# A transformer block on one core: w_up's activations scaled on VectorE, halves evacuated one by one, and new waiting counts

## The chip, the core and the metric

The kernel runs on one core of a Trainium2 chip. A core has a matrix engine (TensorE, PE in the profile, with its weight loads as PEld), VectorE (DVE), ScalarE (ACT), GpSimd (POOL) and SyncE (SP), which issues most of the DMAs. Each engine works through its own list of instructions in order and waits for others by semaphores. The metric is device time in microseconds for one execution; less is better.

## The reference

One block at batch 1, 256 rows, width 1024, all in float32:

```python
h = rms_norm(x, norm_mix_g);  proj = h @ w_in          # pool part u, and q, k, v of 8 heads
x = x + concat([pool_mixer(u), attention(rope(norm(q)), rope(norm(k)), v)]) @ w_out
h = rms_norm(x, norm_xattn_g);  m = rms_norm(mem, norm_mem_g)
x = x + cross_attention(h, m)                          # 4 heads of 256, w_xq, w_xkv, w_xo
h = rms_norm(x, norm_ffn_g)                            # x * rsqrt(mean(x*x) + eps) * g
up = causal_conv3(h @ w_up, conv_w) + conv_b           # w_up: 1024 x 5632, 3 taps along the rows
gate, val = split(up);  x = x + (silu(gate) * val) @ w_down      # 2816 -> 1024
```

## The kernel before

**Precision and tiles.** Every matrix product is done on pairs: a float32 operand is split into a high part, rounded by a copy on ScalarE (`split_h` for weights, `part_h` for activations), and the rest, which VectorE gets by a subtraction (`split_l`, `part_l`). Weights come in units of 128 x 1024; one unit is one output tile of 128 columns over 8 blocks of 128 inputs. `need(u)` is called in front of a unit's matmuls: it emits ScalarE's cast of unit u + look + 1 and VectorE's split of unit u + look; look is 4 while w_up is worked on and 1 in w_down's stage. `b_tile` makes one output tile transposed (128 features x 256 rows): `both` multiplies each block's high weights with both halves of the activation (512 columns) and its low weights with the high half (256 columns), so that a PSUM bank holds two halves that still have to be added. `three` does the same as three matmuls of 256 columns into one half. There are 8 banks.

**The order of work.** Nothing is scheduled by a machine: engines get instructions in the order in which Python emits them. The matmuls are emitted in a straight line, and everything else is in generators (`go` starts one). `tick()` advances every running generator by one `yield`; `b_tile` ticks three times in a tile of 8 blocks, the loops once more after it. The tables WAIT_... at the head of the file say how many ticks a job lets pass between its stages, and so where its instructions stand among the others. `finish(job)` ticks until a job is done.

**w_up and w_down.** 22 pairs (gate tile g = 0, value tile g = 1) make 44 tiles, each 8 blocks. The first 3 pairs use the activations without the row scale 1/rms (`h2`) and are multiplied by it later (`r2b`, a 128 x 256 tile with the scale of each row); from pair SCALED = 3 on the tiles use `hs2`, which `r2_job` makes while the first pairs run: GpSimd multiplies a block of the residual by `r2b`, ScalarE makes the high part and VectorE the low part with the gain g, 8 times. After a pair's two tiles `up_job` copies the second half of each bank on ScalarE (L928) and adds the first half on VectorE (L929), which gives `up`. ScalarE then starts the convolution (`y`, two instructions, L938), VectorE adds the other two taps (four instructions, L945; they are called the taps below), ScalarE takes silu, VectorE multiplies gate and value (L951), and the product is split into `act` (L253 on ScalarE, L259 on VectorE). w_down's tile f then runs over 22 blocks, one for each pair, and waits for that pair's `act`. Its two halves are added to the residual on VectorE (L989) and stored.

**Keys.** `qk_job` turns the projected keys by rope, computes a scale per head (`rsqrt`, a chain on GpSimd), scales the keys on VectorE (L453) and transposes them on TensorE (L460).

Of the kernel before, what the change touches and what calls it, by code (L numbers as in the profile page):

```python
# [13 lines left out]
ALU = mybir.AluOpType  # L14
# [4 lines left out]
S = 256  # L19
# [20 lines left out]
WAIT_MEAN = [0]  # L40
WAIT_STAT = [2, 14, 8, 0, 0, 30]
WAIT_ROPE = [6, 6, 0]
WAIT_QK = [12, 12, 8, 25, 0, 2]
WAIT_V = [2, 10]
WAIT_MEM = [2, 2]
WAIT_SCORE = [5, 4, 0, 9, 1, 6]
# [3 lines left out]
WAIT_R1 = [6]  # L50
WAIT_X = [3, 0, 0, 0, 10, 0, 6, 13, 8]
WAIT_VALUE = [32]
WAIT_R2 = [6, 6, 1, 1, 0]
WAIT_LOW = [2]
WAIT_UP = [6, 2, 5, 7, 9, 8]
SCALED = 3
WARM = 10


C_GMIX, C_X = 0, KT  # L60
# [17 lines left out]
def block_kernel(ctx: ExitStack, tc: tile.TileContext, wpack: bass.AP, xpack: bass.AP, scal: bass.AP,  # L78
# [189 lines left out]
    def three(o, stat, mov, start, stop):  # L268
# [2 lines left out]
        pe.matmul(o, stat[0], mov[1], start=False, stop=False)  # L271
        pe.matmul(o, stat[1], mov[0], start=False, stop=stop)  # L272

    def both(b, stat, mov, start, stop):

        n = mov.shape[1] // 2
        if start:
            pe.matmul(b, stat[0], mov, start=True, stop=False)  # L278
            pe.matmul(b[:, 0:n], stat[1], mov[:, 0:n], start=False, stop=False)  # L279
        else:  # L280
            pe.matmul(b[:, 0:n], stat[1], mov[:, 0:n], start=False, stop=False)  # L281
            pe.matmul(b, stat[0], mov, start=False, stop=stop)  # L282

    def col(t, c):
        return t[:, c:c + 1]
# [80 lines left out]

    def first_splits():
        for k in range(KT):
            part_h(xgv[0][:, k], resid[:, k], col(sc, C_GMIX + k))
            part_l(xgv[1][:, k], resid[:, k], xgv[0][:, k], col(sc, C_GMIX + k))  # L370
            r = slice(k % 2 * 512, k % 2 * 512 + 512)
            split_h(k // 2, r, dve.tensor_copy if k == 0 else act.copy)
            split_l(k // 2, r)
        next_split[0] = FIRST

# [2 lines left out]
    def a_chunk(u0, actv, bk):  # L378

        for k in range(KT):  # L380
            w = need(u0 + k // 2)
            wv = [t[:, (k % 2) * 512:(k % 2) * 512 + 512] for t in w]
            a = [[t[:, k, tt * P:(tt + 1) * P] for t in actv[:2]] for tt in range(TT)]
            for tt in range(TT):
                pe.matmul(bk[tt], a[tt][0], wv[0], start=k == 0, stop=False)  # L385
                pe.matmul(bk[tt], a[tt][1], wv[0], start=False, stop=False)  # L386
            tick()
            for tt in range(TT):
                pe.matmul(bk[tt], a[tt][0], wv[1], start=False, stop=k == KT - 1)  # L389
            tick()  # L390
# [330 lines left out]

    def b_tile(u0, f, blocks, b, mov):

        for k in range(blocks):
            i = f * blocks + k
            w = need(u0 + i // 8)
            wv = [t[:, (i % 8) * P:(i % 8 + 1) * P] for t in w]
            both(b, wv, mov(k), k == 0, k == blocks - 1)
            halves[0] += 1
            if halves[0] % 2 == 0 and k < blocks - 1:  # L730
                tick()
# [168 lines left out]
    def r2_job():  # L900

        yield from wait(WAIT_R2[0])
        v2 = yield from row_mean(acc2, "2")
        r2 = rsqrt(v2, TT, True)
        yield from wait(WAIT_R2[1])
        b = bank()
        for tt in range(TT):
            pe.matmul(b[:, tt * P:(tt + 1) * P], col(r2, tt).to_broadcast([P, P]), ident, start=True, stop=True)
        yield from wait(WAIT_R2[2])
        dve.tensor_copy(r2b, b[:, 0:S])  # L910
        r2_ready.append(True)
        yield from wait(WAIT_R2[3])
        prev = None
        for k in range(KT + 1):
            if prev is not None:
                part_h(hs2[0][:, k - 1], prev, col(sc, C_GFFN + k - 1))
                part_l(hs2[1][:, k - 1], prev, hs2[0][:, k - 1], col(sc, C_GFFN + k - 1))
            if k < KT:
                t = t1(f"hs{k}")
                pool.tensor_tensor(t, resid[:, k], r2b, op=ALU.mult)  # L920
                prev = t
            yield from wait(WAIT_R2[4])

    def up_job(i, bs, scaled):
        src = t2(f"up{i}")
        for g in range(2):
            half = src[:, g * S:(g + 1) * S]
            act.copy(half, bs[g][:, S:])  # L928
            dve.tensor_tensor(half, bs[g][:, 0:S], half, op=ALU.add)  # L929
        if not scaled:  # L930
            while not r2_ready:
                yield
            src2 = src.rearrange("p (g s) -> p g s", g=2)
            dve.tensor_tensor(src2, src2, r2b[:, None, :].to_broadcast([P, 2, S]), op=ALU.mult)
        y = t2(f"y{i}")
        for g in range(2):
            f = i + g * NFF
            act.activation(y[:, g * S:(g + 1) * S], src[:, g * S:(g + 1) * S], AF.Identity, bias=col(sc, C_CB + f),  # L938
                           scale=col(sc, C_CW + 2 * 2 * NFF + f))
        yield from wait(WAIT_UP[1])  # L940
        for j in (1, 2):
            for g in range(2):
                f = i + g * NFF
                uu, yy = src[:, g * S:(g + 1) * S], y[:, g * S:(g + 1) * S]
                dve.scalar_tensor_tensor(yy[:, j:], uu[:, :S - j], col(sc, C_CW + (2 - j) * 2 * NFF + f), yy[:, j:],  # L945
                                         op0=ALU.mult, op1=ALU.add)
        yield from wait(WAIT_UP[2])
        sg = t2(f"sg{i}")
        act.activation(sg[:, 0:S], y[:, 0:S], AF.Silu)
        yield from wait(WAIT_UP[3])  # L950
        dve.tensor_tensor(sg[:, S:], sg[:, 0:S], y[:, S:], op=ALU.mult)  # L951
        yield from wait(WAIT_UP[4])
        h, l = (t[:, i % 8] for t in acts[i // 8][:2])
        part_h(h, sg[:, S:])
        yield from wait(WAIT_UP[5])
        part_l(l, sg[:, S:], h)

    job_r2 = []
    jobs_up = []
    look[0] = LOOKS[10]  # L960
    for i in range(NFF):
        bs = [bank(), bank()]
        if i == 0:
            hs2 = tiles(pair("hs2"), KT, S)
            job_r2.append(go(r2_job()))
        scaled = i >= SCALED
        hv = hs2 if scaled else h2
        if i == SCALED:
            finish(job_r2[0])
        for g in range(2):  # L970
            b_tile(58, 2 * i + g, KT, bs[g], lambda k: hv[2][:, k])
# [10 lines left out]

    look[0] = LOOKS[11]
    for f in range(KT):
        b = bank()
        b_tile(102, f, NFF, b, act_tile)
        o = t2(f"o{f}")[:, 0:S]
        for z, add in enumerate((resid[:, f], o)):
            dve.tensor_tensor(o, b[:, z * S:(z + 1) * S], add, op=ALU.add)  # L989
        nc.sync.dma_start(out[:, f], o)  # L990

# [98 lines left out]
```

## Time and profile before

| | |
|---|---|
| time, median of 3 runs | 390.47 us (390.45 to 392.52) |
| the profiled execution: its time, and the span of its instructions | 390.8 us, 389.0 us |
| TensorE busy | 381.3 us, 98% of the span |
| VectorE busy | 313.3 us, 81% |
| ScalarE busy | 248.2 us, 64% |
| GpSimd busy | 77.1 us, 20% |
| DMA | 69.14 MB, mean 178 GB/s |

The span runs from the first to the last instruction of the profile. Busy time is the union of an engine's instruction times. Instructions of one engine overlap a little, so that two in a row take less than the sum of their durations; the start of one to the start of the next is what the engine can keep up.

### The profile page before, as it was taken

The page shows a single profiled execution, that of the slowest core. Times are in us where ns is not written, and L with a number is a line of the kernel's source. Part 1 is how long each engine was busy: PE and PEld are TensorE (multiplying, and loading weights), DVE is VectorE, ACT ScalarE, POOL GpSimd, SP SyncE. Part 2 cuts the span into 40 slices and gives each one's busy share as a digit, 9 for nine tenths or more (in the row PEclk, how much of TensorE's full clock was granted, in tenths as well). Part 3 has the DMA queues.
Part 4 walks back from the last instruction along what each step waited for, and adds up shares of the span by engine and source line. Part 5 has one row for each costly group of instructions (what it writes and reads, how often), then busy time and mean ns, then how long its engine had stood idle before and what let it go on. Part 6 is the DMA issues. An engine that isn't in the chain of part 4 may idle for free.

```text
span 389.0 us, 5984 instructions
## 1 busy us (share of the span) xinstructions
PE 381.3 (98%) x2178; PEld 328.7 (84%) x2178; DVE 313.3 (81%) x562; ACT 248.2 (64%) x475; POOL 77.1 (20%) x160
## 2 busy tenths in 40 slices
PE   8999899999999999999999999999999999999995
PEld 8888688888888988898888878888888888888884
DVE  4769899978879859678978989999999998654460
ACT  5775797977557747745655678778877777442210
POOL 0272786142832122100325100000000000000000
PEclk9999999999999999999999999999999999999999
DMA  8985381453505624363535055555655554364400
GB/s 281 423 329 192 134 305 67 176 211 110 199 19 216 217 108 190 135 217 109 189 125 231 1 155 204 196 211 209 218 216 202 184 191 181 124 241 166 186 19 21
DMA packets 12269, 69.14 MB, mean 178 GB/s; under 512 B 1360, under 2 KB 2768, under 8 KB 4688
## 3 DMA queue, kind: packets, MB, share of 16 engines
q1 hardware_dynamic: 11952, 68.24, 47.5%
q10 hardware_dynamic: 288, 0.52, 0.4%
q8 instruction: 17, 0.28, 0.3%
q14 instruction: 12, 0.10, 0.1%
HBM read 67.71 MB, written 1.05 MB: 177 GB/s over the span
## 4 chain that ended last, share of the span: by engine, by line
PE 79%; DVE 9%; DMA 3%; ACT 3%; issue 2%; POOL 2%; SPq 0%; DVEq 0%
PE bank L282 34%; PE bank L281 17%; PE bank L385 5%; PE bank L386 5%; PE bank L389 5%; PE bank L278 4%; DVE wl L205 3%; PE bank L279 2%; DMA raw<-wpack 2%; DVE hs L261 2%; DMA sc<-xpack 1%; PE bank L272 1%; PE bank L271 1%; PE bank L270 1%; ACT wh L194 1%
## 5 line engine op out<-in xcount | busy, mean ns | idle before, releaser
L205 DVE TENSOR_TENSOR wl<-raw,wh 128x1024 fp32r<-128x1024 f32 (+1 forms) x126 | 149.3, 1202 | 3.1 <-ACT wh L194 3.1
L194 ACT CAST wh<-raw 128x1024 fp32r<-128x1024 f32 (+1 forms) x125 | 123.6, 1022 | 36.0 <-DMA raw<-wpack 35.0
L282 PE MATMUL bank<-hs,wh 128*128 128x512 f32 x266 | 94.8, 396 | 0.0
L281 PE MATMUL bank<-hs,wl 128*128 128x256 f32 x266 | 74.2, 279 | 0.0
L282 PE MATMUL bank<-act,wh 128*128 128x512 f32 x168 | 59.6, 398 | 0.0
L282 PEld LDWEIGHTS bank<-hs,wh 128*128 128x128 f32 x266 | 49.9, 188 | 10.3
L281 PEld LDWEIGHTS bank<-hs,wl 128*128 128x128 f32 x266 | 50.1, 189 | 1.6
L281 PE MATMUL bank<-act,wl 128*128 128x256 f32 x168 | 47.1, 281 | 0.0
L938 ACT ACTIVATE y<-up,sc 128x256 f32<-128x256 f32 x44 | 24.1, 595 | 27.0 <-DVE up L929 19.7
L282 PEld LDWEIGHTS bank<-act,wh 128*128 128x128 f32 x168 | 31.6, 188 | 7.4
L945 DVE SCALAR_TENSOR_TENSOR y<-up,sc,y 128x255 f32<-128x255 f32 (+1 forms) x88 | 36.6, 477 | 0.3 <-ACT y L938 0.3
L282 PE MATMUL bank<-h,wh 128*128 128x512 f32 x98 | 35.1, 396 | 0.0
L281 PEld LDWEIGHTS bank<-act,wl 128*128 128x128 f32 x168 | 31.7, 189 | 0.3
L281 PE MATMUL bank<-h,wl 128*128 128x256 f32 x98 | 27.6, 281 | 0.0
L989 DVE TENSOR_TENSOR o<-bank,sc 128x256 f32<-128x256 f32 x8 | 3.4, 425 | 29.4 <-PE bank L282 29.4
L385 PE MATMUL bank<-wh,mg 128*128 128x512 f32 x64 | 26.1, 408 | 0.0
L385 PE MATMUL bank<-wh,xg 128*128 128x512 f32 x64 | 26.0, 406 | 0.0
L386 PE MATMUL bank<-wh,xg 128*128 128x512 f32 x64 | 25.4, 397 | 0.0
L386 PE MATMUL bank<-wh,mg 128*128 128x512 f32 x64 | 25.1, 392 | 0.0
L747 POOL TENSOR_TENSOR h_acc<-h_sq,h_acc 128x256 f32<-128x256 f32 x14 | 13.4, 956 | 43.3 <-ACT h_sq L746 43.1
L282 PEld LDWEIGHTS bank<-h,wh 128*128 128x128 f32 x98 | 18.4, 188 | 3.6
L255 ACT ACTIVATE h<-sc 128x256 fp32r<-128x256 f32 x16 | 8.2, 511 | 20.5 <-DVE sc L739 20.4
(256 smaller groups left out, 770.1 us busy)
## 6 DMA issues: line engine op xcount, KB each, us to landing
raw<-wpack SPq DMA_DIRECT2D x59, 1024.0 KB, 4.8
raw<-wpack SPq DMA_DIRECT2D x4, 512.0 KB, 7.8
mraw<-memT SPq DMA_DIRECT2D x4, 256.0 KB, 6.8
out<-o SPq DMA_DIRECT2D x8, 128.0 KB, 1.9
raw<-wpack ACTq DMA_DIRECT2D x2, 256.0 KB, 3.5
raw<-wpack SPq DMA_DIRECT2D x2, 256.0 KB, 4.8
sc<-xpack SPq DMA_DIRECT2D x1, 512.0 KB, 6.4
tab<-table SPq DMA_DIRECT2D x1, 480.0 KB, 9.1
```

The costliest lines, as they stand in the source:

```text
L194: copy(split[u][0][:, r], unit(u)[:, r])
L205: dve.tensor_tensor(l[:, r], unit(u)[:, r], h[:, r].bitcast(F32), op=ALU.subtract)
L255: act.activation(h, src, AF.Copy, scale=scale)
L278: pe.matmul(b, stat[0], mov, start=True, stop=False)
L281: pe.matmul(b[:, 0:n], stat[1], mov[:, 0:n], start=False, stop=False)
L282: pe.matmul(b, stat[0], mov, start=False, stop=stop)
L385: pe.matmul(bk[tt], a[tt][0], wv[0], start=k == 0, stop=False)
L386: pe.matmul(bk[tt], a[tt][1], wv[0], start=False, stop=False)
L389: pe.matmul(bk[tt], a[tt][0], wv[1], start=False, stop=k == KT - 1)
L747: pool.tensor_tensor(acc, sq, acc, op=ALU.add)
L938: act.activation(y[:, g * S:(g + 1) * S], src[:, g * S:(g + 1) * S], AF.Identity, bias=col(sc, C_CB + f), scale=col(sc, C_CW + 2 * 2 * NFF ...
L945: dve.scalar_tensor_tensor(yy[:, j:], uu[:, :S - j], col(sc, C_CW + (2 - j) * 2 * NFF + f), yy[:, j:], op0=ALU.mult, op1=ALU.add)
```

## The change

It has six parts. (1) In the first splits the cast of a weight part stands ahead of the activation's low part, the first projection's matmuls alternate between the two banks, and 8 instead of 10 idle matmuls warm TensorE. (2) The keys are scaled 3 ticks later and transposed 5 ticks later. (3) `r2_job` makes hs2's products on VectorE, with scale and gain in one instruction, in pairs of blocks; ScalarE and VectorE then split 512 columns at once. (4) Each half of a pair is evacuated by a generator of its own, `up_half`, as soon as its tile is done, and VectorE's addition stands two ticks behind ScalarE's copy. (5) `up_job` starts 2 ticks later and its taps come 3 ticks after `y` instead of 2; the last three pairs have short pauses. (6) w_down's last tile uses `three`, so that one addition is left at the end.

```diff
-WAIT_QK = [12, 12, 8, 25, 0, 2]
+WAIT_QK = [12, 14, 11, 25, 0, 2]
-WAIT_R2 = [6, 6, 1, 1, 0]
+WAIT_R2 = [6, 6, 1, 0, 1]
-WAIT_UP = [6, 2, 5, 7, 9, 8]
+WAIT_UP = [6, 3, 5, 7, 9, 8]
+WAIT_LAST = [0, 1, 2, 1, 2, 1]
+N_LAST = 3
-WARM = 10
+WARM = 8
...
+            split_h(k // 2, r, dve.tensor_copy if k == 0 else act.copy)
             part_l(xgv[1][:, k], resid[:, k], xgv[0][:, k], col(sc, C_GMIX + k))
-            split_h(k // 2, r, dve.tensor_copy if k == 0 else act.copy)
             split_l(k // 2, r)
...
             for tt in range(TT):
                 pe.matmul(bk[tt], a[tt][0], wv[0], start=k == 0, stop=False)
+            for tt in range(TT):
                 pe.matmul(bk[tt], a[tt][1], wv[0], start=False, stop=False)
...
-        prev = None
-        for k in range(KT + 1):
-            if prev is not None:
-                part_h(hs2[0][:, k - 1], prev, col(sc, C_GFFN + k - 1))
-                part_l(hs2[1][:, k - 1], prev, hs2[0][:, k - 1], col(sc, C_GFFN + k - 1))
-            if k < KT:
-                t = t1(f"hs{k}")
-                pool.tensor_tensor(t, resid[:, k], r2b, op=ALU.mult)
-                prev = t
-            yield from wait(WAIT_R2[4])
+        for j in range(KT // 2):
+            ts.append(t2(f"hs{j}").rearrange("p (k s) -> p k s", k=2))
+            for k in range(2):
+                dve.scalar_tensor_tensor(ts[j][:, k], resid[:, 2 * j + k], col(sc, C_GFFN + 2 * j + k), r2b,
+                                         op0=ALU.mult, op1=ALU.mult)
+            part_h(hs2[0][:, 2 * j:2 * j + 2], ts[j])
+        yield from wait(WAIT_R2[4])
+        for j in range(KT // 2):
+            part_l(hs2[1][:, 2 * j:2 * j + 2], ts[j], hs2[0][:, 2 * j:2 * j + 2])
...
+    def up_half(o, b):
+        act.copy(o, b[:, S:])
+        yield from wait(WAIT_LOW[0])
+        dve.tensor_tensor(o, b[:, 0:S], o, op=ALU.add)
+
+    def up_job(i, src, scaled):
+        pause = WAIT_LAST if i >= NFF - N_LAST else WAIT_UP
+        yield from wait(WAIT_LOW[0])
-        src = t2(f"up{i}")
-        for g in range(2):
-            half = src[:, g * S:(g + 1) * S]
-            act.copy(half, bs[g][:, S:])
-            dve.tensor_tensor(half, bs[g][:, 0:S], half, op=ALU.add)
...
         for g in range(2):
-            b_tile(58, 2 * i + g, KT, bs[g], lambda k: hv[2][:, k])
+            b = bank()
+            b_tile(58, 2 * i + g, KT, b, lambda k: hv[2][:, k])
+            go(up_half(up[:, g * S:(g + 1) * S], b))
             if g == 0:
                 tick()
-        jobs_up.append(go(up_job(i, bs, scaled)))
+        jobs_up.append(go(up_job(i, up, scaled)))
         tick()
...
-        b = bank()
-        b_tile(102, f, NFF, b, act_tile)
+        last = f == KT - 1
+        b = bank()[:, 0:S] if last else bank()
+        b_tile(102, f, NFF, b, (lambda k: halves_of(act_tile(k))) if last else act_tile)
```

**VectorE in w_up's stage.** One pair's worth of VectorE's list in the middle of the stage, before (`up` is the pair's sum of halves, `wl` a split of weights, `y` the taps, `sg` the gated product, `act` its low part; the numbers tell buffers apart):

```order
L929 TENSOR_TENSOR up_2650<-bank_2596,up_2650 128x256
L929 TENSOR_TENSOR up_2650<-bank_2597,up_2650 128x256
L205 TENSOR_TENSOR wl_2662<-raw_2502,wh_2625 128x1024
L945 SCALAR_TENSOR_TENSOR y_2655<-up_2650,sc,y_2655 128x255 x2
L945 SCALAR_TENSOR_TENSOR y_2655<-up_2650,sc,y_2655 128x254 x2
L205 TENSOR_TENSOR wl_2688<-raw_2502,wh_2660 128x1024
L951 TENSOR_TENSOR sg_2640<-sg_2640,y_2593 128x256
L259 TENSOR_TENSOR act_2311<-sg_2517,act_2311 128x256
```

The same stretch in the changed kernel:

```order
L935 TENSOR_TENSOR up_2575<-bank_2576,up_2575 128x256
L961 TENSOR_TENSOR sg_2586<-sg_2586,y_2528 128x256
L208 TENSOR_TENSOR wl_2640<-raw_2490,wh_2612 128x1024
L262 TENSOR_TENSOR act_2313<-sg_2464,act_2313 128x256
L935 TENSOR_TENSOR up_2575<-bank_2609,up_2575 128x256
L955 SCALAR_TENSOR_TENSOR y_2651<-up_2575,sc,y_2651 128x255 x2
L955 SCALAR_TENSOR_TENSOR y_2651<-up_2575,sc,y_2651 128x254 x2
L208 TENSOR_TENSOR wl_2676<-raw_2490,wh_2638 128x1024
```

The instructions are the same ten. Before, a weight split stood between the second addition and the taps; now the taps stand directly behind the second addition, and both splits lie elsewhere. ScalarE's `y` stands between addition and taps in the dependencies, in both kernels.

**VectorE where hs2 is made.** Before, from the copy of `r2b` on (six more hs rows follow, then the taps of pair 0):

```order
L205 TENSOR_TENSOR wl_2346<-raw_2160,wh_2319 128x1024
L910 COPY r2b<-bank_2339 128x256
L934 TENSOR_TENSOR up_2312<-up_2312,r2b 128x512
L261 SCALAR_TENSOR_TENSOR hs_2245<-hs_2361,sc,hs_2245 128x256
L261 SCALAR_TENSOR_TENSOR hs_2245<-hs_2365,sc,hs_2245 128x256
```

And in the changed kernel:

```order
L918 COPY r2b<-bank_2338 128x256
L925 SCALAR_TENSOR_TENSOR hs_2353<-sc,r2b 128x256 x2
L925 SCALAR_TENSOR_TENSOR hs_2357<-sc,r2b 128x256 x2
L925 SCALAR_TENSOR_TENSOR hs_2361<-sc,r2b 128x256 x2
L925 SCALAR_TENSOR_TENSOR hs_2365<-sc,r2b 128x256 x2
L944 TENSOR_TENSOR up_2241<-up_2241,r2b 128x512
L935 TENSOR_TENSOR up_2314<-bank_2315,up_2314 128x256
L262 TENSOR_TENSOR hs_2242<-hs_2353,hs_2242 128x2x256
L262 TENSOR_TENSOR hs_2242<-hs_2357,hs_2242 128x2x256
```

The eight products now stand on VectorE itself, and the low parts are four instructions of 512 columns (two more follow) instead of eight of 256.

**VectorE at the keys.** Before (`m1k` are the keys, `rs1y` their scale, `m2q` a product of the queries' rope):

```order
L205 TENSOR_TENSOR wl_416<-raw_244,wh_396 128x1024
L226 TENSOR_SCALAR rs2y<-vx 128x2
L453 TENSOR_TENSOR m1k_271<-m1k_271,rs1y 128x512
L453 TENSOR_TENSOR m1k_276<-m1k_276,rs1y 128x512
L427 TENSOR_TENSOR m2q_385<-bank_281,ropeq 128x8x32 x2
L427 TENSOR_TENSOR m2q_390<-bank_282,ropeq 128x8x32 x2
L205 TENSOR_TENSOR wl_456<-raw_299,wh_414 128x1024
```

And now:

```order
L208 TENSOR_TENSOR wl_414<-raw_242,wh_394 128x1024
L229 TENSOR_SCALAR rs2y<-vx 128x2
L434 TENSOR_TENSOR m2q_383<-bank_279,ropeq 128x8x32 x2
L434 TENSOR_TENSOR m2q_388<-bank_280,ropeq 128x8x32 x2
L208 TENSOR_TENSOR wl_452<-raw_297,wh_412 128x1024
L460 TENSOR_TENSOR m1k_269<-m1k_269,rs1y 128x512
L460 TENSOR_TENSOR m1k_274<-m1k_274,rs1y 128x512
```

The keys' scaling has moved behind the queries' four products and a weight split. On TensorE the keys' transposes stand 16 matmuls of 512 columns later than before, two matmuls ahead of the queries'.

## Rows read from the trace of the kernel before

**Rows 1.** Waits of TensorE: engine line, waited for: total us, times, longest.

```profile
PE bank L460 <- DVE m1k L453: 1.4, 1, 1.4
PE bank L279 <- DVE wl L205: 1.0, 1, 1.0
```

**Rows 2.** Windows: stretch, length, busy us (PE, PEld, DVE, ACT, POOL), PEclk, DMA share, GB/s.

```profile
240.00:324.00 84.00, 84.00 (x482) 73.16 (x482) 84.00 (x163) 66.48 (x130) 0.00 (x0) 1.00 0.55 201
```

**Rows 3.** Timeline, VectorE and ScalarE, one pair: start us, us, what, [idle <-releaser].

```profile
313.88 0.75 DVE L929 TENSOR_TENSOR up<-bank,up 128x256 f32<-128x256 f32 x2
314.33 1.10 ACT L938 ACTIVATE y<-up,sc 128x256 f32<-128x256 f32 x2 [1.05 <-DVE up L929]
315.68 1.66 DVE L945 SCALAR_TENSOR_TENSOR y<-up,sc,y 128x255 f32<-128x255 f32 x4
319.06 0.75 DVE L929 TENSOR_TENSOR up<-bank,up 128x256 f32<-128x256 f32 x2
```

**Rows 4.** Timeline of several engines, from hs2's making to pair 3's taps.

```profile
208.58 7.06 POOL L920 TENSOR_TENSOR hs<-sc,r2b 128x256 f32<-128x256 f32 x8 [7.60 <-DVE r2b L910]
210.79 5.92 DVE L261 SCALAR_TENSOR_TENSOR hs<-hs,sc,hs 128x256 fp32r<-128x256 f32 x8 [1.56 <-ACT hs L255]
220.35 0.40 PE L278 MATMUL bank<-hs,wh 128*128 128x512 f32 x1
225.03 0.76 DVE L929 TENSOR_TENSOR up<-bank,up 128x256 f32<-128x256 f32 x2 [1.50 <-ACT up L928]
227.70 0.38 PE L279 MATMUL bank<-hs,wl 128*128 128x256 f32 x1 [0.96 <-DVE wl L205]
232.74 1.67 DVE L945 SCALAR_TENSOR_TENSOR y<-up,sc,y 128x255 f32<-128x255 f32 x4
```

**Rows 5.** Timeline where w_up ends: last pair, and w_down's first tile.

```profile
322.92 0.40 PE L278 MATMUL bank<-act,wh 128*128 128x512 f32 x1
324.70 1.09 ACT L938 ACTIVATE y<-up,sc 128x256 f32<-128x256 f32 x2 [1.05 <-DVE up L929]
325.33 1.77 DVE L945 SCALAR_TENSOR_TENSOR y<-up,sc,y 128x255 f32<-128x255 f32 x4 [0.34 <-ACT y L938]
328.02 1.09 DVE L259 TENSOR_TENSOR act<-sg,act 128x256 fp32r<-128x256 f32 x3
329.17 0.28 PE L281 MATMUL bank<-act,wl 128*128 128x256 f32 x1
```

**Rows 6.** Timeline of several engines at the keys.

```profile
40.40 0.61 PE L389 MATMUL bank<-wl,xg 128*128 128x512 f32 x2
41.46 0.22 POOL L236 TENSOR_TENSOR rs1y<-rs1t,rs1y 128x16 f32<-128x16 f32 x1
41.71 1.30 DVE L453 TENSOR_TENSOR m1k<-m1k,rs1y 128x512 f32<-128x512 f32 x2 [1.80 <-POOL rs1y L236]
42.46 1.32 PE L460 MATMUL bank<-tab,m1k 128*128 128x128 f32 x8 [1.44 <-DVE m1k L453]
```

**Rows 7.** Groups of instructions: the additions; busy us, mean ns, idle before.

```profile
L929 DVE TENSOR_TENSOR up<-bank,up 128x256 f32<-128x256 f32 x44 | 16.5, 415 | 1.5 <-ACT up L928 1.5
```

**Rows 8.** Timeline of the first matmuls and of the third block's cast.

```profile
5.36 0.77 PE L385 MATMUL bank<-wh,xg 128*128 128x512 f32 x1
7.90 0.61 ACT L194 CAST wh<-raw 128x512 fp32r<-128x512 f32 x1
9.07 0.39 PE L385 MATMUL bank<-wh,xg 128*128 128x512 f32 x1
```

**Rows 9.** Timeline: one block of `three` elsewhere, and the kernel's last additions.

```profile
174.36 0.28 PE L270 MATMUL bank<-xpt,vx 128*128 128x256 f32 x1
174.72 0.40 PE L278 MATMUL bank<-ox,wh 128*128 128x512 f32 x1
385.12 0.42 DVE L989 TENSOR_TENSOR o<-bank,sc 128x256 f32<-128x256 f32 x1 [5.74 <-PE bank L282]
385.57 0.42 DVE L989 TENSOR_TENSOR o<-bank,o 128x256 f32<-128x256 f32 x1
```

More of the change, by code (lines that the diff above doesn't have):

```diff
@@ L272, in three, with halves_of @@
         pe.matmul(o, stat[1], mov[0], start=False, stop=stop)
+    def halves_of(t):
+        return [t[:, 0:S], t[:, S:]]
     def both(b, stat, mov, start, stop):
@@ L368, in first_splits @@
         for k in range(KT):
+            r = slice(k % 2 * 512, k % 2 * 512 + 512)
             part_h(xgv[0][:, k], resid[:, k], col(sc, C_GMIX + k))
+            split_h(k // 2, r, dve.tensor_copy if k == 0 else act.copy)
             part_l(xgv[1][:, k], resid[:, k], xgv[0][:, k], col(sc, C_GMIX + k))
-            r = slice(k % 2 * 512, k % 2 * 512 + 512)
-            split_h(k // 2, r, dve.tensor_copy if k == 0 else act.copy)
             split_l(k // 2, r)
@@ L722, in b_tile @@
     def b_tile(u0, f, blocks, b, mov):
+        product = both if b.shape[1] > S else three
         for k in range(blocks):
@@ L727, in b_tile @@
             wv = [t[:, (i % 8) * P:(i % 8 + 1) * P] for t in w]
-            both(b, wv, mov(k), k == 0, k == blocks - 1)
+            product(b, wv, mov(k), k == 0, k == blocks - 1)
             halves[0] += 1
@@ L912, in r2_job @@
         yield from wait(WAIT_R2[3])
-        prev = None
-        for k in range(KT + 1):
-            if prev is not None:
-                part_h(hs2[0][:, k - 1], prev, col(sc, C_GFFN + k - 1))
-                part_l(hs2[1][:, k - 1], prev, hs2[0][:, k - 1], col(sc, C_GFFN + k - 1))
-            if k < KT:
-                t = t1(f"hs{k}")
-                pool.tensor_tensor(t, resid[:, k], r2b, op=ALU.mult)
-                prev = t
-            yield from wait(WAIT_R2[4])
-    def up_job(i, bs, scaled):
-        src = t2(f"up{i}")
-        for g in range(2):
-            half = src[:, g * S:(g + 1) * S]
-            act.copy(half, bs[g][:, S:])
-            dve.tensor_tensor(half, bs[g][:, 0:S], half, op=ALU.add)
+        ts = []
+        for j in range(KT // 2):
[14 more added lines that the diff above has]
+        yield from wait(WAIT_LOW[0])
         if not scaled:
@@ L939, in up_job @@
                            scale=col(sc, C_CW + 2 * 2 * NFF + f))
-        yield from wait(WAIT_UP[1])
+        yield from wait(pause[1])
         for j in (1, 2):
@@ L946, in up_job @@
                                          op0=ALU.mult, op1=ALU.add)
-        yield from wait(WAIT_UP[2])
+        yield from wait(pause[2])
         sg = t2(f"sg{i}")
         act.activation(sg[:, 0:S], y[:, 0:S], AF.Silu)
-        yield from wait(WAIT_UP[3])
+        yield from wait(pause[3])
         dve.tensor_tensor(sg[:, S:], sg[:, 0:S], y[:, S:], op=ALU.mult)
-        yield from wait(WAIT_UP[4])
+        yield from wait(pause[4])
         h, l = (t[:, i % 8] for t in acts[i // 8][:2])
         part_h(h, sg[:, S:])
-        yield from wait(WAIT_UP[5])
+        yield from wait(pause[5])
         part_l(l, sg[:, S:], h)
@@ L961, in block_kernel @@
     for i in range(NFF):
-        bs = [bank(), bank()]
+        up = t2(f"up{i}")
         if i == 0:
@@ L984, in block_kernel @@
     for f in range(KT):
-        b = bank()
-        b_tile(102, f, NFF, b, act_tile)
+        last = f == KT - 1
+        b = bank()[:, 0:S] if last else bank()
+        b_tile(102, f, NFF, b, (lambda k: halves_of(act_tile(k))) if last else act_tile)
         o = t2(f"o{f}")[:, 0:S]
-        for z, add in enumerate((resid[:, f], o)):
+        for z, add in enumerate((resid[:, f], o)[:1 if last else 2]):
             dve.tensor_tensor(o, b[:, z * S:(z + 1) * S], add, op=ALU.add)
```

## Prediction

> **What bounds the kernel now.** I read TensorE's waits first, since TensorE is busy for 98% of the span. The view has two waits behind its first instruction: 1.4 us at the keys' transposes and 1.0 us for a weight split early in w_up [rows 1]. So a faster helper can win little: those two waits, something at the start, something behind the last matmul, 3 to 4 us in all. What can be lost is larger, and the next view says where. Over most of w_up VectorE is busy for 84.00 of 84.00 us, while TensorE does 482 matmuls, 32 to a pair: 84.00 / 482 x 32 = 5.58 us a pair [rows 2]. VectorE's own pace is 319.06 - 313.88 = 5.18 us a pair [rows 3]. An engine that is quicker than the one it serves and still never rests is working off a debt.
>
> The timeline shows the debt. Pair 3's second tile ends at 220.35, and its taps start at 232.74, 12.4 us later [rows 4]. The last pair's second tile ends at 322.92 and its taps start at 325.33, 2.4 us later, and there VectorE waits for the first time, 0.34 us for ScalarE's `y` [rows 5]. Gaining 5.58 - 5.18 = 0.40 us a pair (and TensorE's own stalls) it caught up just in time: the last low parts are done at 328.02 + 1.09 = 329.11, while w_down's first tile, with 22 blocks from 322.92 on at (329.17 - 322.92) / 18 = 0.347 us, reaches block 18 at 329.17 [rows 5]. That is the spare of the whole stage. The question of this change is therefore what it adds to or takes from VectorE's list between hs2 and w_down.
>
> **The change, part by part.**
>
> *hs2 on VectorE.* Removed is the 1.56 us in which VectorE waited for the first product and ScalarE's cast, and eight low parts that took 5.92 us, 0.74 each, while GpSimd's eight products ran beside them for 7.06 us [rows 4]. Added are eight products; the nearest row is the taps, the same operation on 255 columns, 1.66 / 4 = 0.415 us each [rows 3], so 3.3 us. The four low parts of 512 columns cost as the keys' scaling, 1.30 / 2 = 0.65 us [rows 6], so 2.6 us. 5.9 us for 5.92: nothing, and the wait of 1.56 us is gone. VectorE's wait of 1.50 us for ScalarE's copy of pair 2 [rows 4] goes too, since the halves are copied as their tiles end. The Trainium skill, Perfetto Trace Analysis, section Optimizing Scalar/DVE Operations, speaks against this part: work of a saturated VectorE may be worth offloading, even to GpSimd, and here it comes back. By that rule the products would be a pure addition, 3.3 us more on VectorE, and the time some 3 us above my sum. The row shows why I do not follow it: the low parts beside GpSimd took 0.74 us instead of about 0.42.
>
> *Taps directly behind the second addition.* Both kernels do the same ten instructions for a pair, but before a split of weights stood between the additions and the taps, as long as ScalarE needed for `y`. Now nothing stands there. The first half's `y` can be made early. The second half's cannot: ScalarE started `y` at 314.33, and the first addition had ended at 313.88 + 0.415 = 314.30 [rows 3, 7], so 0.03 us behind its addition; from the start of `y` to taps that wait for it are 325.33 - 324.70 = 0.63 us [rows 5]. So the taps of the second half can start 0.66 us after the addition's end. The tap of the first half covers 0.415 of this, and 0.08 less if instructions overlap as the two additions do (0.75 us for two of 0.415) [rows 3, 7]. Exposed are 0.25 to 0.33 us a pair; I take 0.33. With it a pair takes 5.51 us on VectorE against TensorE's 5.58: the debt is hardly paid back any more. For the 19 pairs from 3 to 21 that is 6.3 us. Behind this wait stand the next weight split, additions and low parts, and TensorE waits for them. In pairs 1 and 2 the scaling by `r2b` comes between addition and `y`, so both halves are exposed: 0.66 + 0.08 in one, 0.4 in the other where a product stands between, 1.15 us together.
>
> *The end of w_up.* The short pauses put a product behind silu and a low part behind its cast with little between. No row shows such a pair of steps; each is bounded by nothing and by the 0.66 us of the `y` step. Three of them, partly covered: 0.9 us (0.3 to 1.5). The last low part in VectorE's list is now that of pair 18, which block 18 of w_down's first tile needs.
>
> *Sum for the stage.* Waits removed: 1.56 + 1.50 + 0.34 = 3.4. Added: 1.15 + 6.3 + 0.9 = 8.35. VectorE's last low part comes 4.95 us later, at 334.1 instead of 329.11, and block 18, which ran at 329.17, goes at about 334.1: **+4.9 us**. That TensorE no longer waits 0.96 us for the split at 227.70 [rows 4] changes nothing here: it only arrives earlier and stands longer.
>
> *Keys.* VectorE stood from 41.71 - 1.80 = 39.91 on for a scale that GpSimd finished at 41.68, and TensorE stood 1.44 us for the scaled keys [rows 6]. Now VectorE first does four products, 1.66 us by the taps' price, and a split, 315.68 - (313.88 + 0.75) = 1.05 us [rows 3]; it scales from 42.6 to 43.9. TensorE comes to the transposes 16 matmuls later, 40.86 + 16 x 0.23 = 44.5 (0.23 as 0.61 for two of 0.39) [rows 6]. The wait goes: **-1.4 us**, with 0.6 us to spare; 0 if the queries' transposes, two matmuls behind, or the scores, which need both copies, take its place.
>
> *Start.* Earlier casts and two idle matmuls fewer start TensorE up to 0.7 us sooner, but the third block's cast ends at 7.90 + 0.61 = 8.51 and TensorE is there at 9.07 [rows 8]: between 0 and 0.5, I take **-0.3 us**.
>
> *Last tile.* One addition less, 385.57 - 385.12 = 0.45; three matmuls a block take 174.72 - 174.36 = 0.36 [rows 9] instead of 0.35, 22 times 0.01: **-0.25 us**.
>
> Together 4.9 - 1.4 - 0.3 - 0.25 = +2.95 us. The profiled execution took 390.8, which gives 393.75; it stands 0.33 over the median, so against 390.47 I predict **393.4 us**. With 0.25 to 0.42 us a pair, 0.3 to 1.5 at the end and the keys' gain between 0 and 1.4 this case reaches from 391.3 to 395.6.
>
> **The rivals.**
>
> *Faster (0.19): the taps' wait is covered, and VectorE catches up as before.* For it: 0.07 us a pair still separate 5.51 from 5.58, and every other part takes work or waits away. Against: the additions and taps are neighbours in the list, and `y` lies between them. Then w_down's first tile does not wait, and TensorE also keeps the 1.0 us of [rows 1]: -1.4 - 1.0 - 0.3 - 0.25 = -2.95, 387.5 us. It decides below 0.17 us of exposed wait a pair: there VectorE's delay is 1.95 us and the gains are eaten up exactly.
>
> *No change (0.17): half of it is covered*, 0.17 us a pair: 390.4 us (388.6 to 391.3).
>
> *Slower still (0.12).* In my forecast TensorE stands some 6 us in w_down's first tile, and no wait of this trace is longer than 1.44 us [rows 6]. PEclk is 1.00 [rows 2], but the first real matmul took 0.77 us where later ones take 0.39 [rows 8], and that phase ended before 9.07. If a stretch like it followed the long stall, at half the pace for 5 us, it would cost 2.5 us more: 395.9 us. The Trainium skill, TensorE: Matmul & The Clock Gate, section The HAM clock gate, has such a rule: idleness brings the clock down to 1.2 GHz. No stall here is long enough to show it. A new wait at the scores, in the keys' place, would end near 394.8.
>
> *The change does not do what its words say.* "Convolution behind the next split" is not what the list shows: the taps went from behind a split to in front of one. This is the main case itself.
>
> **How the numbers follow.** The forecast has 0.52, the rivals 0.19, 0.17 and 0.12. The likeliest case alone reaches from 391.3 to 395.6. A range from 387.7 to 396.0 leaves out about half of the fast rival and half of the slow one, less than 2 in 10. Half a per cent is 1.95 us, about what this measurement can tell from no change: below 388.5 faster, 0.19; above 392.4 slower, 0.12 and some four fifths of the forecast's, 0.55; between, 0.26.
>
> **What would show it.** Right: a wait of TensorE for `act` in w_down's first tile, of 5 to 7 us over two or three blocks near 327 to 334; VectorE's taps waiting on ScalarE's `y` about 20 times, 0.25 to 0.4 us each; a pair on VectorE about 5.5 us; no wait at the keys and for splits; no GpSimd work for hs2. Wrong: w_down's first tile without a wait, or VectorE idle in w_up with the lag of pair 10 already down to 3 us; a TensorE wait for the scores near 49; PEclk under 1.00 in w_down.

## The result, and the profile after

The changed kernel takes 395.95 us (395.48 to 396.31) against 390.56 us (390.45 to 392.52) in the same runs: 1.0125 times as long, with a 95% interval of 1.0091 to 1.016. The forecast was 393.4 with a range to 396.0 and most of the chance on slower: the time lies 2.55 us above the forecast and 0.05 us inside the range. In the profiled executions the time went from 390.8 to 395.48, 4.7 us. One caution for later comparisons: the kernel before took 390.1 to 391.4 us in executions with a mean granted clock of 0.998 or more and 391.7 to 392.5 us in those with 0.996 or less, so its median differs from one set of runs to the next; where it comes from is told below.

TensorE's waits after the change (the same view as [rows 1]):

```profile
PE bank L288 <- DVE act L262: 6.7, 2, 3.5
...
PE bank L467 <- DVE m1q L439: 0.4, 1, 0.4
```

The waits for the keys and for a split are gone. In their place stand 6.7 us, in two pieces, for the low parts of `act`, where no such wait was before, and a small new one for the queries. The timeline of TensorE in w_down's first tile shows them. `both` has two instructions that bear on it: L287 needs only a pair's high part, L288 its low part too.

```profile
324.92 0.27 PE L287 MATMUL bank<-act,wl 128*128 128x256 f32 x1
328.45 0.50 PE L288 MATMUL bank<-act,wh 128*128 128x512 f32 x1 [3.26 <-DVE act L262]
328.79 0.28 PE L287 MATMUL bank<-act,wl 128*128 128x256 f32 x1
332.54 0.79 PE L288 MATMUL bank<-act,wh 128*128 128x512 f32 x1 [3.46 <-DVE act L262]
...
333.34 0.63 PE L288 MATMUL bank<-act,wh 128*128 128x512 f32 x1
...
336.31 0.28 PE L287 MATMUL bank<-act,wl 128*128 128x256 f32 x1
336.43 0.40 PE L288 MATMUL bank<-act,wh 128*128 128x512 f32 x1
```

Block 17 waits 3.26 us and runs, and then block 18 waits 3.46 us. Then something else begins: the 512-column matmul that takes 0.40 us at 336.43 takes 0.63 at 333.34. The windows (columns as in [rows 2]) give the granted clock, 0.69 on average from 330 to 340, so part of that stretch ran at the lower of TensorE's two levels, 1.2 instead of 2.4 GHz (called half pace below):

```profile
320.00:330.00 10.00, 5.81 (x32) 4.56 (x31) 9.38 (x21) 7.26 (x15) 0.00 (x0) 0.97 0.51 168
330.00:340.00 10.00, 7.46 (x33) 6.49 (x34) 6.11 (x10) 5.67 (x7) 0.00 (x0) 0.69 0.20 64
340.00:350.00 10.00, 10.00 (x60) 8.75 (x59) 4.25 (x5) 2.00 (x2) 0.00 (x0) 1.00 0.61 228
```

Why the low parts are late is seen on VectorE and ScalarE, in the steady pair that answers to [rows 3]:

```profile
306.01 0.42 DVE L935 TENSOR_TENSOR up<-bank,up 128x256 f32<-128x256 f32 x1
306.34 0.48 DVE L955 SCALAR_TENSOR_TENSOR y<-up,sc,y 128x255 f32<-128x255 f32 x1
307.10 1.27 DVE L955 SCALAR_TENSOR_TENSOR y<-up,sc,y 128x255 f32<-128x255 f32 x3 [0.28 <-ACT y L948]
...
311.56 0.42 DVE L935 TENSOR_TENSOR up<-bank,up 128x256 f32<-128x256 f32 x1
```

```profile
306.46 0.60 ACT L948 ACTIVATE y<-up,sc 128x256 f32<-128x256 f32 x1 [1.40 <-DVE up L935]
```

The second addition, one tap of the first half, and then a hole until ScalarE, which could only start on the second half at 306.46, has made its `y`. From addition to addition it is 311.56 - 306.01 = 5.55 us, where before it was 5.18, and TensorE's pair takes 5.58. VectorE's waits count how often:

```profile
DVE y L955 <- ACT y L948: 6.2, 21, 0.7
```

Early w_up, for [rows 4], has lost GpSimd's work and the waits of 1.56 and 1.50 us, and got the two waits in pairs 1 and 2:

```profile
206.54 3.26 DVE L925 SCALAR_TENSOR_TENSOR hs<-sc,r2b 128x256 f32<-128x256 f32 x8
...
210.65 2.49 DVE L262 TENSOR_TENSOR hs<-hs,hs 128x512 fp32r<-128x512 f32 x4
...
217.58 1.76 DVE L955 SCALAR_TENSOR_TENSOR y<-up,sc,y 128x255 f32<-128x255 f32 x4 [0.67 <-ACT y L948]
...
223.68 1.77 DVE L955 SCALAR_TENSOR_TENSOR y<-up,sc,y 128x255 f32<-128x255 f32 x4 [0.33 <-ACT y L948]
```

The end of w_up, for [rows 5]: three short waits, and the last low part done at 331.72 + 0.76 = 332.48, just ahead of block 18's matmul at 332.54:

```profile
329.40 1.27 DVE L955 SCALAR_TENSOR_TENSOR y<-up,sc,y 128x255 f32<-128x255 f32 x3 [0.20 <-ACT y L948]
330.82 0.43 DVE L961 TENSOR_TENSOR sg<-sg,y 128x256 f32<-128x256 f32 x1 [0.15 <-ACT sg L959]
331.72 0.76 DVE L262 TENSOR_TENSOR act<-sg,act 128x256 fp32r<-128x256 f32 x2 [0.47 <-ACT act L256]
```

The keys, for [rows 6], and the one addition left at the end, for [rows 9]:

```profile
42.43 1.29 DVE L460 TENSOR_TENSOR m1k<-m1k,rs1y 128x512 f32<-128x512 f32 x2 [0.40 <-POOL rs1y L239]
43.78 1.03 PE L467 MATMUL bank<-tab,m1k 128*128 128x128 f32 x8
46.17 0.66 PE L467 MATMUL bank<-tab,m1q 128*128 128x128 f32 x4 [0.45 <-DVE m1q L439]
390.08 0.42 DVE L1002 TENSOR_TENSOR o<-bank,sc 128x256 f32<-128x256 f32 x1 [5.89 <-PE bank L275]
```

### The profile page after: what moved, and what is told of

It reads as the page before. It is cut to its first block, busy times and chain, and to the rows that moved or that the text cites. A ratio compares the mean times of both kernels' runs of the same rounds, so it can differ in the third digit from the quotient of the medians.

```text
span 393.5 us, 6033 instructions
## 1 busy us (share of the span) xinstructions
PE 381.6 (97%) x2196; PEld 330.1 (84%) x2196; DVE 314.4 (80%) x565; ACT 247.3 (63%) x471; POOL 70.9 (18%) x152
## 4 chain that ended last, share of the span: by engine, by line
PE 52%; DVE 33%; ACT 6%; DMA 3%; issue 3%; POOL 2%; SPq 0%; DVEq 0%; ACTq 0%
PE bank L288 18%; DVE wl L208 14%; PE bank L287 9%; DVE y L955 6%; PE bank L391 4%; PE bank L393 4%; PE bank L396 4%; DVE up L935 4%; ACT y L948 3%; DMA raw<-wpack 2%; DVE act L262 2%; DVE sg L961 2%; PE bank L284 2%; PE bank L275 2%; PE bank L274 2%
## 5 line engine op out<-in xcount | busy, mean ns | idle before, releaser
L197 ACT CAST wh<-raw 128x1024 fp32r<-128x1024 f32 (+1 forms) x125 | 126.0, 1026 | 38.6 <-DMA raw<-wpack 34.6
L288 PE MATMUL bank<-hs,wh 128*128 128x512 f32 x266 | 94.8, 396 | 0.0
L287 PE MATMUL bank<-hs,wl 128*128 128x256 f32 x266 | 74.2, 279 | 0.0
L288 PE MATMUL bank<-act,wh 128*128 128x512 f32 x147 | 53.5, 406 | 6.7 <-DVE act L262 6.7
L288 PEld LDWEIGHTS bank<-hs,wh 128*128 128x128 f32 x266 | 49.9, 188 | 10.3
L287 PEld LDWEIGHTS bank<-hs,wl 128*128 128x128 f32 x266 | 50.1, 189 | 1.7
L948 ACT ACTIVATE y<-up,sc 128x256 f32<-128x256 f32 x44 | 26.0, 598 | 28.6 <-DVE up L935 23.6
L287 PE MATMUL bank<-act,wl 128*128 128x256 f32 x147 | 41.7, 284 | 0.0
L288 PEld LDWEIGHTS bank<-act,wh 128*128 128x128 f32 x147 | 28.3, 192 | 13.8 <-DVE act L262 7.4
L288 PE MATMUL bank<-h,wh 128*128 128x512 f32 x98 | 35.1, 395 | 0.0
L287 PEld LDWEIGHTS bank<-act,wl 128*128 128x128 f32 x147 | 28.4, 193 | 0.4
L287 PE MATMUL bank<-h,wl 128*128 128x256 f32 x98 | 27.6, 281 | 0.0
L288 PEld LDWEIGHTS bank<-h,wh 128*128 128x128 f32 x98 | 18.4, 188 | 3.6
L391 PE MATMUL bank<-wh,mg 128*128 128x512 f32 x64 | 20.9, 408 | 0.0
L391 PE MATMUL bank<-wh,xg 128*128 128x512 f32 x64 | 20.7, 405 | 0.1
L288 PE MATMUL bank<-cat,wh 128*128 128x512 f32 x56 | 20.0, 394 | 0.0
L288 PE MATMUL bank<-ox,wh 128*128 128x512 f32 x56 | 20.0, 396 | 0.0
```

The source lines that it names most:

```text
L197: copy(split[u][0][:, r], unit(u)[:, r])
```

## The experiments

**Taps a tick later.** The theory: the hole between second addition and taps makes VectorE late. One number puts a split of weights into it.

```diff
-WAIT_UP = [6, 3, 5, 7, 9, 8]
+WAIT_UP = [6, 4, 5, 7, 9, 8]
```

> The changed kernel with the taps four ticks behind `y` instead of three, so that a split of weights stands between a pair's second addition and its taps again; nothing else differs. Theory (the exposed `y` is what delays VectorE): of the 21 waits of 0.3 to 0.7 us for ScalarE's `y` in w_up nearly none is left, a pair takes VectorE about 5.2 us instead of 5.55, its last low part comes some 6 us earlier than 332.48, and TensorE's waits of 6.7 us for `act` shrink to between 0 and 1.5. The granted clock in w_down's first tile stays at 1.00. The time is 387.0 to 389.0 us. Rival A (the separate evacuation of the halves, or the products on VectorE, cost VectorE the time): the waits for `y` go but a pair still takes 5.4 us or more and the stall stays above 4 us; 393 us or more. Rival B (the short stages of the last three pairs make the stall): the pace of VectorE improves, but TensorE still stands 3 to 6 us before block 18; 391 to 394 us.

Measured: 387.22 us (386.79 to 387.9), 0.9887 of the kernel before (0.9858 to 0.9916). VectorE's timeline:

```profile
301.90 1.66 DVE L955 SCALAR_TENSOR_TENSOR y<-up,sc,y 128x255 f32<-128x255 f32 x4
...
307.08 1.66 DVE L955 SCALAR_TENSOR_TENSOR y<-up,sc,y 128x255 f32<-128x255 f32 x4
...
324.64 0.76 DVE L262 TENSOR_TENSOR act<-sg,act 128x256 fp32r<-128x256 f32 x2 [0.47 <-ACT act L256]
```

No taps wait; a pair takes 307.08 - 301.90 = 5.18 us again; the last low part is done at 325.40, 7.1 us earlier; TensorE has no wait in w_down and a clock of 1.00 throughout. Both rivals fall: the halves' evacuation and the short pauses are still there. One place in a list is worth 8.7 us.

**The same place, in the kernel before.**

```diff
-WAIT_UP = [6, 2, 5, 7, 9, 8]
+WAIT_UP = [6, 1, 5, 7, 9, 8]
```

> The kernel before with the taps one tick behind `y` instead of two and nothing else, which puts them directly behind both additions, with no split between: the suspected cost alone, without the other five parts. Here the two `y` are made from additions that stand next to each other. Theory: 20 waits for ScalarE's `y` of 0.3 to 0.7 us a pair appear, VectorE needs 5.5 to 5.9 us a pair instead of 5.18, TensorE waits for `act` in w_down's first tile, 5 us or more, and the clock falls behind it as in the changed kernel: 396 to 402 us against 390.5. Rival (the order of additions, `y` and taps is covered, and another part of the change brings the delay): fewer than 5 such waits, no stall, within 1 us of the kernel before.

Measured: 402.58 us, 1.0275 times the kernel before (1.024 to 1.0309). VectorE, and TensorE's waits:

```profile
299.92 0.75 DVE L929 TENSOR_TENSOR up<-bank,up 128x256 f32<-128x256 f32 x2
301.01 1.76 DVE L945 SCALAR_TENSOR_TENSOR y<-up,sc,y 128x255 f32<-128x255 f32 x4 [0.34 <-ACT y L938]
...
305.63 0.75 DVE L929 TENSOR_TENSOR up<-bank,up 128x256 f32<-128x256 f32 x2
```

```profile
PE bank L282 <- DVE act L259: 3.9, 2, 2.8
...
PE bank L279 <- DVE wl L205: 2.5, 1, 2.5
```

A pair takes 5.71 us, more than TensorE's 5.58; the lag grows. So the cost alone, without the rest of the change, does it. Two details were expected otherwise: the waits for `act` are 3.9 us instead of 5 or more, and the time lies 0.6 us above the range. Not all of the 12 us is waiting for `act`: TensorE also waits 2.5 us for a split of weights (1.0 before), and the granted clock is 0.83 from 220 to 230 and 0.85 and 0.80 in the two slices from 330 to 350. Note that the row shows a wait of 0.34 us where the pair grew by 0.53. A row's wait is only the idle time; the four taps also take 1.76 us instead of 1.66, and at the gap the overlap of two instructions in a row is lost (0.08 us for the two additions of [rows 3, 7]).

**Without the short pauses.**

```diff
-N_LAST = 3
+N_LAST = 0
```

> The changed kernel without the short pauses of the last three pairs; they go through the same stages as all others. Theory (VectorE is late by its list, whatever the end looks like): the stall stays, 5 to 7 us, now before a later block (19 to 21) of w_down's first tile; the time is within 1.5 us of 395.9. Rival B (the short stages put exposed steps into the end and make the stall): the stall falls below 3 us and the clock stays at 1.00; 391 us or less.

Measured: 393.47 us (392.56 to 394.31), between the two expectations, 2.5 us below the changed kernel. TensorE and VectorE at the end:

```profile
326.85 0.50 PE L288 MATMUL bank<-act,wh 128*128 128x512 f32 x1 [1.95 <-DVE act L262]
...
329.79 0.80 PE L288 MATMUL bank<-act,wh 128*128 128x512 f32 x1 [2.33 <-DVE act L262]
```

```profile
329.32 0.41 DVE L262 TENSOR_TENSOR act<-sg,act 128x256 fp32r<-128x256 f32 x1
...
329.99 1.09 DVE L262 TENSOR_TENSOR act<-sg,act 128x256 fp32r<-128x256 f32 x3
```

VectorE finishes at 331.08 instead of 332.48: the short pauses cost 1.4 us where VectorE is late. They also put the low part of pair 18 last, which w_down needs three blocks before the end. Here it is done at 329.32 + 0.41 = 329.73, 2.75 us before 332.48. The waits sum to 4.3 instead of 6.7 us, less than the 5 to 7 expected, and they stand before blocks 17 and 18 again and not before a later one. So the stall does not need the pauses, but they lengthen it.

**Matmuls in the stall.** Here VectorE is left as it is, and TensorE gets something to do while it waits.

```diff
+            if u0 == 102 and f == 0 and k in (17, 18):
+                fill = bank()
+                for _ in range(14):
+                    pe.matmul(fill[:, 0:P], idle, idle, start=True, stop=True)
```

> The changed kernel with 14 more matmuls of 128 columns, into a bank that nothing reads, ahead of block 17 and again ahead of block 18 of w_down's first tile, so that TensorE's two long waits begin behind them and are shorter. VectorE's work is untouched. Theory (half pace follows TensorE's standing still): the last low part is still done near 332.5 and block 18 starts near 332.6, but the granted clock in the slice from 330 to 340 is over 0.95 instead of 0.69 and matmuls of 0.39 us follow at once; the time is 1.4 to 2.5 us less, 393.4 to 394.5. Rival (the slow matmuls have another cause, power or contention for one, not the standing still): the clock falls as before, and the time is 395.9 or more by what the added matmuls cost, up to 1 us.

Measured: 394.05 us (393.74 to 394.27). TensorE's timeline and the window:

```profile
328.71 3.29 PE L736 MATMUL bank<-idle 128*128 128x128 f32 x28
331.76 0.36 PE L287 MATMUL bank<-act,wl 128*128 128x256 f32 x1
332.45 0.50 PE L288 MATMUL bank<-act,wh 128*128 128x512 f32 x1 [0.33 <-DVE act L262]
...
332.91 0.40 PE L288 MATMUL bank<-act,wh 128*128 128x512 f32 x1
```

```profile
330.00:340.00 10.00, 9.67 (x62) 8.50 (x62) 6.03 (x10) 5.56 (x7) 0.00 (x0) 1.00 0.31 101
```

The 14 added matmuls ahead of a block show as 28 records. Block 18 still starts at 332.45, and the next matmuls take 0.40 us. So 1.9 us of the changed kernel's time (395.95 - 394.05, medians) are the half pace behind the stall, and they follow TensorE's standing still, not the stall's other effects. The two timelines give about the same: from block 18 to the matmul that starts at 336.43 it is 336.43 - 332.54 = 3.89 us, and to the same matmul here 334.65 - 332.45 = 2.20, 1.7 us less.

**The keys alone**: the one line of WAIT_QK in the kernel before.

> The kernel before with the keys' scaling and transposes of the changed kernel and nothing else. Theory (the wait of 1.44 us at the keys' transposes is replaced by none or by the 0.45 us at the queries' that the changed kernel has): everything behind it comes 1.0 to 1.5 us earlier, VectorE's debt in w_up included; the time is 1.0 to 1.5 us under the kernel before, and the last low part still arrives just in time. Rival (the later work has slack, or the scores wait instead): within 0.4 us of the kernel before.

Measured: 389.4 us (388.93 to 389.86), 0.9943 (0.9922 to 0.9965), 1.2 us under the median of all those runs of the kernel before whose clock was 0.998 or more (390.6), as expected. But against the whole median of these runs, 391.89, it is 2.5 us, and none of its six executions had a clock under 0.998.

**The products alone**: hs2's making in the kernel before as in the changed one.

> The kernel before with the changed making of hs2 (its products on VectorE, 512 columns a low part) and nothing else. Theory by the rows (eight low parts beside GpSimd cost what eight products and four low parts cost without it): no GpSimd work there, VectorE is about 1.5 us less behind for pair 3, TensorE's wait of 0.96 us for a split is gone, w_down's first tile does not wait: 0.7 to 1.3 us under the kernel before. Rival, by the rule that work should go off a saturated VectorE: VectorE is 1.7 us more behind (3.3 us of products less the wait of 1.56), and since before had no spare at block 18 of w_down's first tile TensorE waits there about as long: 1.0 to 2.0 us over the kernel before.

Measured: 389.49 us (388.79 to 391.38), 0.9946 (0.9926 to 0.9966). The rule's rival falls: VectorE's products and low parts take the same 3.26 and 2.49 us as in the changed kernel, no wait appears in w_down, and the early splits no longer hold TensorE. The gain is larger than I expected, which the run of the start, keys and last tile below settles. The profiled execution was one of the long ones, and it shows where: TensorE at the keys, and the window behind.

```profile
43.28 1.32 PE L460 MATMUL bank<-tab,m1k 128*128 128x128 f32 x8 [1.81 <-DVE m1k L453]
...
45.20 0.63 PE L385 MATMUL bank<-wh,xg 128*128 128x512 f32 x1
...
48.08 0.40 PE L386 MATMUL bank<-wh,xg 128*128 128x512 f32 x1
```

```profile
45.00:50.00 5.00, 5.00 (x17) 3.94 (x17) 4.97 (x10) 3.29 (x8) 3.33 (x7) 0.70 0.00 2
```

Behind the keys' wait the clock fell, as behind the stall of the changed kernel.

**Matmuls at the keys**, in the kernel before, ahead of the transposes that wait:

```diff
+        if n == "k":
+            fill = bank()
+            for _ in range(10):
+                pe.matmul(fill[:, 0:P], idle, idle, start=True, stop=True)
```

> The kernel before with ten more matmuls of 128 columns, into a bank that nothing reads, ahead of the keys' transposes, where TensorE stands 1.44 us (1.81 us in the kernel with the products alone, whose clock fell to 0.70 from 45 to 50). Nothing waits less: the transposes still start when VectorE has scaled the keys. Theory (standing still there brings TensorE to half pace in some executions, and that is why the times of the kernel before lie between 390.2 and 392.5 at clocks of 1.000 down to 0.993): all times lie within 1 us of each other, at clocks of 0.998 to 1.000, with a median of 390.2 to 390.8. Rival (the clock falls for another reason, or elsewhere): times and clocks are spread as those of the kernel before, or all are later by up to 1 us.

Measured: 391.18 us (390.76 to 392.12). The 12 executions all have clocks of 0.998 to 1.000; of the 45 of the kernel before whose clock is on record 25 lie at 0.996 or less, each over 391.6 us. So the clock's part of the theory holds. Its times do not: they spread over 1.4 us instead of 1, and the median misses by 0.4 us. Three of the twelve took 391.8 to 392.1 us at a clock of 0.999 or more, so a long execution is not always one of a lower clock. In the profiled execution, the longest of them, TensorE reaches the keys 0.4 us later than in [rows 6], after a wait for a weight's cast at the start, and the added matmuls end later than the first scaled keys arrive; how much of the 0.4 us is due to either was not settled.

**Start, keys and last tile**, in the kernel before (parts 1, 2 and 6 of the change).

> The kernel before with the start, the keys and the last tile of the changed kernel; hs2's products are on GpSimd and w_up is as before. Theory (the parts add up): 0.5 to 0.8 us less than with the keys alone (389.4), of it 0.3 to 0.5 at the first matmuls and 0.25 to 0.31 behind the last block; 388.6 to 388.9 us. The difference to the kernel with hs2's products on VectorE beside these parts (387.04) is then 1.6 to 1.9 us, what the products alone bring. Rival (the start's gain is lost again at the keys or in w_up, where VectorE has no spare): 389.1 to 389.4.

Measured: 388.84 us (388.35 to 389.69), 0.6 under the keys alone, as expected if the parts add up; the spreads of the two overlap. Beside it stands

**w_up as before**, which is the same with hs2's products on VectorE (parts 1, 2, 3 and 6):

> The changed kernel with w_up's evacuation, its jobs and their pauses as before: what is left of the change is the start, the keys, hs2's products on VectorE and the last tile. Theory: 2.0 us from the start and the keys, 1.0 to 1.9 from the splits early in w_up, 0.3 from the last tile, and VectorE a pair in 5.2 us as before, so that w_down's first tile waits for at most 0.5 us: 386.5 to 388.0 us. Rival (TensorE, now 3.9 us earlier, outruns VectorE's debt also without the exposed `y`): a wait of 1 to 3 us at block 18 or later, and 388.5 to 391 us.

Measured: 387.04 us (386.72 to 387.56), with no wait in w_down. The products are worth 388.84 - 387.04 = 1.8 us, about twice the wait of 0.96 us in [rows 1]. The timelines agree: from the first matmul on hs2 to w_down's first TensorE takes 320.78 - 212.61 = 108.17 us with GpSimd's products and 319.55 - 213.31 = 106.24 with VectorE's, 1.93 less. The rest stood in another view, the waits of the weight loads (PEld). In the kernel with GpSimd's products, from 200 to 330:

```profile
PEld bank L282 <- DVE wl L205: 2.4, 3, 1.4
```

Three late splits, 2.4 us: 0.55, 1.39 and 0.43. The longest ends at the same matmul as TensorE's own wait of 0.96; 0.55 + 0.96 + 0.43 = 1.94 us. With the products on VectorE this view has no row in that stretch.

**Taps a tick later, without the short pauses** (WAIT_UP[1] = 4, N_LAST = 0).

> The changed kernel with the taps one tick later and without the short pauses of the last three pairs. Theory (with VectorE in time the end of w_up doesn't matter): no wait in w_down's first tile, clock 1.00, and the time is that of the kernel with the taps a tick later alone, 387.2 us, within 0.5. Rival (the short pauses cost 2.5 us as they did where VectorE was late, or gain by bringing the last low parts forward): 386.5 or less, or a wait at block 21 and 388 or more.

Measured: 386.85 us (386.57 to 387.82), 0.9885 (0.9863 to 0.9907), the same within the spread. With VectorE in time the pauses neither cost nor bring anything.

**Queries two ticks later** on top of that, for the small new wait:

```diff
-WAIT_QK = [12, 14, 11, 25, 0, 2]
+WAIT_QK = [14, 14, 11, 25, 0, 2]
```

> The changed kernel with the taps a tick later, no short pauses, and the queries' transposes two ticks later, where TensorE still waits 0.5 us for the queries. Theory (TensorE's waits are all that is left to win): that wait goes, nothing takes its place, 386.3 to 386.6 us against 386.85. Rival (the scores come two ticks later too, and softmax with all behind it): a new wait of about 0.5 us or more later on, 386.8 us or above.

Measured: 386.67 us (386.31 to 387.06), 0.9877 (0.9851 to 0.9904). The queries' wait is gone and 0.2 us for a split is new. The median is 0.2 us lower, which these runs can't tell from nothing. It is the fastest median of all kernels here; four of them (386.67 to 387.22) can't be told apart.

## Why the prediction was right, and where its size was off

*Taps directly behind the second addition.* Right, and shown both ways: the hole taken out of the changed kernel gives back 8.7 us, put into the kernel before it costs 12.0 against its 390.6. Its size was 5.55 - 5.18 = 0.37 us a pair, 0.33 forecast. The waits for `y` are 21, where about 20 were forecast.

*hs2 on VectorE.* Right in sign. Eight products took 3.26 us (3.3 forecast) and four low parts 2.49 (2.6), and the waits of 1.56 and 1.50 us went. The prediction held that TensorE's wait of 0.96 us, won back, changes nothing at the end, since TensorE then only stands longer there. No run tests that where VectorE is late; where it is in time, the products are worth 1.8 us. One by one, the second to the seventh low part in the kernel before start 0.88 us apart, in step with GpSimd's products (also 0.88 apart); most of them take 0.95 us, and the last, which starts behind GpSimd's end, takes 0.47. Of the rule in the Trainium skill, Perfetto Trace Analysis, section Optimizing Scalar/DVE Operations, the runs show the opposite case: here work that came from GpSimd to a full VectorE made VectorE quicker. The same section adds that offloading between these two might not help, and that agrees with 0.74 us a low part beside GpSimd's work [rows 4] against 2.49 / 4 = 0.62 for twice the columns without it.

*The end of w_up.* 0.20 + 0.15 + 0.47 = 0.82 us of waits, 0.9 forecast; taken away whole, the short pauses gave VectorE 1.4 us and the low part of block 18 2.75. The difference is their new order of the low parts, which the prediction named and gave no term.

*The stall.* VectorE's last low part was forecast 4.95 us later by w_up, less 1.7 for keys and start: 3.25. It came 332.48 - 329.11 = 3.37 later. TensorE stood 6.7 us over two blocks, forecast 5 to 7 over two or three. One reading behind the forecast was wrong: the kernel before does not reach w_down just in time. All its pairs have the same pauses, so its last four low parts are those of pairs 18 to 21 in this order, and block 18's is the first of them:

```profile
327.35 0.42 DVE L259 TENSOR_TENSOR act<-sg,act 128x256 fp32r<-128x256 f32 x1
329.28 0.39 PE L282 MATMUL bank<-act,wh 128*128 128x512 f32 x1
```

It is done at 327.77, 1.5 us before it is used; the last, done at 329.11, belongs to block 21, which uses it at 330.32. The sum still came out, because in the changed kernel the short pauses put block 18's low part last, and so it is late against 329.28 by all of VectorE's delay.

*Keys, start, last tile.* TensorE's instructions from 116 to 220 us lie 2.0 us earlier than before, forecast 1.7; the last tile gave 0.3, forecast 0.25. Of the keys' wait of 1.44 us 0.45 came back at the queries, one of the places that the prediction had named. One thing was not seen: the keys' wait also brought the clock down in about half of the executions, so removing it also takes about 1.6 us from those (the middles of the two groups are 390.6 and 392.2). The prediction took no stall of this kernel for long enough to show that; in the one execution profiled the clock indeed stayed up.

*The range.* The upper end of the forecast case is added up wrongly. With 0.42 us a pair and 1.5 at the end the terms give 395.7 with the keys' gain and 397.1 without it; the stated 395.6 leaves the second out.

*What was mis-sized* is the sum's missing term, which the prediction had as a rival of 0.12, slower still: half pace behind the long stall. I had priced it at 2.5 us, for 5 us at half pace, a length that no row gave; the slow matmuls lasted 3.8 us (332.54 to 336.31), and with matmuls in the stall 1.9 us came back. PEclk under 1.00 in w_down stood among the signs that the prediction is wrong, and it came. From the rows: block 18 came 3.25 us later than before (332.54 against 329.17 + 0.12, the step from L287 to L288 at 336.31), the end of the span 4.5; with the 0.3 us that the last tile gives, 1.6 us came in between. The forecast case and this rival were not alternatives: the stall of the one is the condition of the other. 2.95 + 1.6 is nearly the 4.7 us between the profiled executions. Between the medians it is 0.7 us more: 0.5 from two executions of the changed kernel with a clock of 0.987 instead of 0.991, the rest because the profiled execution of before lay above its median. That the rival's 395.9 lies so near the measured 395.95 is partly luck, since its price was too high; and the range holds the result only because it was drawn to take in half of this rival. The Trainium skill, TensorE: Matmul & The Clock Gate, section The HAM clock gate, says that idleness throttles the array; the rows agree, with 0.63 us for a matmul of 0.40.

What stays open: why the changed kernel's executions differ (0.987 and 0.991), since only one of them was profiled, and why some executions of the kernel before keep the full clock behind the same wait.

## What to carry to other kernels

Before a count in a table is changed, look at what stands between a result and its user in the user engine's list: a filler of 1.2 us between two instructions that hand work to another engine and back hid 0.37 us, 20 times. Where a helper engine is only 7% quicker than the one it serves (5.18 against 5.58 us), add its waits up over the whole stage and find the first consumer that has no spare. And when a forecast has the matrix engine standing for microseconds, put the lower clock behind the stall into the sum and not into the rivals; matmuls that nothing reads, put into the stall, got that part back (1.9 us).

## What the runs showed that I had not expected

- A wait of 1.4 to 1.8 us at the keys makes the same program run in two groups of clocks, with times of 390.1 to 391.4 and 391.7 to 392.5 us. One long execution that was profiled, of the kernel with the products alone, shows matmuls of 0.63 us from 44.36 to 47.76; ten idle matmuls in that wait left only the first group's clock, though not only its times.
- The wait in a row understates the loss: 0.28 us shown, 0.37 lost a pair; 0.34 shown, 0.53 lost in the kernel before with the taps at once.
- Late weights show on the weight loads (2.4 us in three waits) more than on the matmuls (1.0 us in one).
